# Batch norm and ReLU on one core: 32 KB runs on one queue in place of 4 KB rows on two

## Chip, core and metric

The kernel runs on one core of a Trainium2 chip. The metric is the device time of one execution in microseconds (us). Shown are the median of 13 runs and, for the views of the profile, one profiled execution.

## The reference

The input x has 32 images of 128 channels of 32 x 32 floats: 16.78 MB in, as much out. Each channel has four parameters.

```python
normalized = (x - running_mean[None, :, None, None]) / np.sqrt(running_var[None, :, None, None] + eps)
scaled = normalized * gamma[None, :, None, None] + beta[None, :, None, None]
return np.maximum(scaled, 0).astype(np.float32)
```

With scale = gamma / sqrt(var + eps) and bias = beta - mean x scale, each value becomes relu(scale x value + bias), with one scale and one bias per channel.

## The kernel before

The channel is the partition: 128 channels, 128 partitions. Two images make a tile `t` of 128 x 2 x 1024 floats (1 MB), so there are 16 tiles, and as many buffers (`BUFS`): no buffer is used twice. In DRAM a row of 1024 floats (4 KB) is one image and channel; the 128 channels of an image are neighbours, and the next image lies 512 KB further. So for each partition a tile is two separate runs of 4 KB.

The order of the work is the order of the program on each engine, and each engine that issues DMAs has a queue of its own.

- gpsimd (POOL in the profile) issues four loads of the parameter vectors, 512 bytes each, into the single row `prow` (L63 to L66).
- sync (SP) issues the load of tile 0 in two halves, and, in the main loop, those of the tiles 2, 4, 6 and 8 to 15. scalar (ACT) issues tiles 1, 3, 5 and 7 first of all, tile 1 in two halves. All of them go through `emit_input` (L53, the DMA at L58).
- TensorE turns each parameter row into a column of 128 partitions with a matmul against a single 1.0 (L79); ScalarE takes the square root (L89), and VectorE makes `scale_t` and `bias_t`, 128 x 1 each (L97 to L103).
- ScalarE then does one activation per tile of 128 x 2048 (L138) and issues that tile's store itself (L145). Tile 0 is cut finer: its first image in pieces of 256 and 768 columns, its second image whole, each with its own store (`relu_store`, L109 and L118).

A scale or bias operand of an activation is one column of 128 values, one per partition, and holds for the whole row of that instruction.

Of the kernel before, what the change touches and what calls it, by code (L numbers as in the profile page):

```python
# [1 line left out]

# [4 lines left out]


@with_exitstack
def kernel(  # L10
    ctx: ExitStack,
    tc: tile.TileContext,
    x: bass.AP,
    gamma: bass.AP,
    beta: bass.AP,
    running_mean: bass.AP,
    running_var: bass.AP,
    eps: bass.AP,
    out: bass.AP,
):  # L20
    nc = tc.nc

    B, C, H, W = x.shape
    HW = H * W
    assert C == nc.NUM_PARTITIONS, f"expected {nc.NUM_PARTITIONS} channels, got {C}"

    x3 = x.rearrange("b c h w -> b c (h w)")
    out3 = out.rearrange("b c h w -> b c (h w)")

    f32 = mybir.dt.float32  # L30

    NBMAX = 2
    n_tiles = B // NBMAX
    sizes = [NBMAX] * n_tiles
    scalar_tiles = (1, 3, 5, 7)
    splits = {0: 2, 1: 2}
    BUFS = 16
    SEPARATE_PSUM = True
    FIRST_PIECES = (256, HW - 256)

    params = ctx.enter_context(tc.tile_pool(name="params", bufs=1))
    eps_t = params.tile([C, 1], f32)
    nc.vector.memset(eps_t, float(eps))  # L43
    prow = params.tile([1, 4 * C], f32)
    one_t = params.tile([1, 1], f32)
    nc.vector.memset(one_t, 1.0)  # L46

    data = ctx.enter_context(tc.tile_pool(name="data", bufs=BUFS))
    tiles = {}
    for i in (0,) + scalar_tiles:  # L50
        tiles[i] = data.tile([C, NBMAX, HW], f32, name="t")

    def emit_input(i, t, engine):  # L53
        nsp = splits.get(i, 1)
        step = NBMAX // nsp
        b0 = i * NBMAX
        for j in range(nsp):
            engine.dma_start(  # L58
                out=t[:, j * step : (j + 1) * step],
                in_=x3[b0 + j * step : b0 + (j + 1) * step].transpose([1, 0, 2]),  # L60
            )

    nc.gpsimd.dma_start(out=prow[0:1, 3 * C : 4 * C], in_=running_var[None, :])  # L63
    nc.gpsimd.dma_start(out=prow[0:1, 0 * C : 1 * C], in_=gamma[None, :])  # L64
    nc.gpsimd.dma_start(out=prow[0:1, 2 * C : 3 * C], in_=running_mean[None, :])  # L65
    nc.gpsimd.dma_start(out=prow[0:1, 1 * C : 2 * C], in_=beta[None, :])  # L66

    emit_input(0, tiles[0], nc.sync)
    for i in scalar_tiles:
        emit_input(i, tiles[i], nc.scalar)  # L70

    pp = ctx.enter_context(tc.tile_pool(name="pp", bufs=1, space=bass.MemoryType.PSUM))
    if SEPARATE_PSUM:
        pcols = [pp.tile([C, 1], f32, name=f"p{k}") for k in range(4)]
    else:
        pc = pp.tile([C, 4], f32)
        pcols = [pc[:, k : k + 1] for k in range(4)]
    for k in (3, 0, 2, 1):
        nc.tensor.matmul(  # L79
            pcols[k],  # L80
            prow[0:1, k * C : (k + 1) * C],
            one_t[0:1, 0:1],
            start=True,
            stop=True,
        )
    g_col, b_col, mu_col, var_col = pcols

    std_t = params.tile([C, 1], f32)
    nc.scalar.activation(  # L89
        out=std_t,  # L90
        in_=var_col,
        func=mybir.ActivationFunctionType.Sqrt,
        bias=eps_t[:, 0:1],
        scale=1.0,
    )
    rstd_t = params.tile([C, 1], f32)
    nc.vector.reciprocal(out=rstd_t, in_=std_t)  # L97
    scale_t = params.tile([C, 1], f32)
    nc.vector.tensor_mul(out=scale_t, in0=g_col, in1=rstd_t)  # L99
    ms_t = params.tile([C, 1], f32)  # L100
    nc.vector.tensor_mul(out=ms_t, in0=mu_col, in1=scale_t)  # L101
    bias_t = params.tile([C, 1], f32)
    nc.vector.tensor_sub(out=bias_t, in0=b_col, in1=ms_t)  # L103

    out_ring = {}
    n_out = [0]

    def relu_store(t, b, img, c0, c1):
        nc.scalar.activation(  # L109
            out=t[:, img : img + 1, c0:c1],  # L110
            in_=t[:, img : img + 1, c0:c1],
            func=mybir.ActivationFunctionType.Relu,
            bias=bias_t[:, 0:1],
            scale=scale_t[:, 0:1],
        )
        eng = out_ring.get(n_out[0], nc.scalar)
        n_out[0] += 1
        eng.dma_start(  # L118
            out=out3[b : b + 1, :, c0:c1].transpose([1, 0, 2]),
            in_=t[:, img : img + 1, c0:c1],  # L120
        )

    for i, nb in enumerate(sizes):
        b0 = i * NBMAX
        if i in tiles:
            t = tiles.pop(i)
        else:
            t = data.tile([C, NBMAX, HW], f32, name="t")
            emit_input(i, t, nc.sync)
        if i == 0:  # L130
            c0 = 0
            for w in FIRST_PIECES:
                relu_store(t, b0, 0, c0, c0 + w)
                c0 += w
            for img in range(1, nb):
                relu_store(t, b0 + img, img, 0, HW)
        else:
            nc.scalar.activation(  # L138
                out=t[:, :nb],
                in_=t[:, :nb],  # L140
                func=mybir.ActivationFunctionType.Relu,
                bias=bias_t[:, 0:1],
                scale=scale_t[:, 0:1],
            )
            nc.scalar.dma_start(out=out3[b0 : b0 + nb].transpose([1, 0, 2]), in_=t[:, :nb])  # L145


# [1 line left out]
_INS = ['x', 'gamma', 'beta', 'running_mean', 'running_var', 'eps']  # L149
_OUTS = [((32, 128, 32, 32), 'float32')]  # L150
#: Inputs that are plain numbers.
_NUMBERS = {'eps': 1e-05}


# [26 lines left out]
```

## Time and profile before

| | us |
|---|---|
| median of 13 runs (lowest, highest) | 86.53 (86.44, 86.95) |
| the profiled execution, its whole time | 86.53 |
| its span, first to last event of the core | 84.7 |
| ScalarE, 15 activations of 128 x 2048, mean of one | 2.084 |
| loads issued by SP and by ACT | 13 and 5 |
| stores issued by ACT | 18 |

How to read the page: busy times of the engines are shares of the span; two lines then cut the span into 40 slices of 2.1 us, with the busy share of the 16 DMA engines in tenths and the GB/s that they moved. The windows view gives the same for any stretch of the span. Queue q1 is SP's, q10 ACT's, q0 gpsimd's. A packet is one piece of a transfer as one DMA engine handles it. "us to landing" is the time from the issue of a DMA to its completion. A share above 1 of the DMA engines' time means that records of neighbouring packets overlap.

### The profile page before, as it was taken

Reading aid. Unit: us, or ns where it says so; the run is one execution under the profiler, and the core shown is the slowest. Engines: PE = TensorE matmul, PEld = TensorE weight load, DVE = VectorE, ACT = ScalarE, POOL = GpSimd, SP = SyncE. Lnnn points to the kernel's source line nnn. Section 1 sums busy time; section 2 is a strip of 40 time slices with the busy share of each in tenths; the row PEclk is TensorE's granted clock in tenths of the full one; section 3 lists DMA queues with packets and bytes.
Section 4 is the critical chain, followed back from the end, with each engine's and each line's share of the span. In section 5 each row is a group of like instructions: output and inputs, shape, how many; then the busy total and the mean of one; then the engine's idle time right before and its main releaser. Section 6 shows DMA issues by size and latency. Waiting matters only on the chain.

```text
span 84.7 us, 153 instructions
## 1 busy us (share of the span) xinstructions
PE 2.3 (3%) x8; PEld 2.0 (2%) x8; DVE 0.7 (1%) x6; ACT 34.8 (41%) x20; POOL 2.3 (3%) x8
## 2 busy tenths in 40 slices
PE   0006400000000000000000000000000000000000
PEld 0005300000000000000000000000000000000000
DVE  0001100000000000000000000000000000000000
ACT  0411479007920890000049597793978910000000
POOL 5500000000000000000000000000000000000000
DMA  1999999999999999999999999999999999999991
GB/s 23 363 408 366 420 416 420 412 414 410 402 369 420 418 421 422 421 421 420 421 423 418 423 421 420 423 420 420 423 418 425 418 420 421 421 421 418 423 423 56
DMA packets 9025, 33.57 MB, mean 396 GB/s; under 512 B 704, under 2 KB 832, under 8 KB 9024
## 3 DMA queue, kind: packets, MB, share of 16 engines
q10 hardware_dynamic: 5616, 20.97, 60.8%
q1 hardware_dynamic: 3280, 12.58, 37.0%
q0 software_dynamic: 128, 0.00, 0.1%
q14 instruction: 1, 0.01, 0.0%
HBM read 16.78 MB, written 16.78 MB: 396 GB/s over the span
## 4 chain that ended last, share of the span: by engine, by line
DMA 65%; ACT 7%; ACTq 4%; issue 3%
DMA t<-in_x_dram 65%; ACT t L138 7%; ACTq L58 2%; ACTq L145 2%
## 5 line engine op out<-in xcount | busy, mean ns | idle before, releaser
L138 ACT ACTIVATE t<-t,bias_t,scale_t 128x2048 f32<-128x2048 f32 x15 | 30.6, 2084 | 24.6 <-DMA t<-in_x_dram 22.3
L109 ACT ACTIVATE t<-t,bias_t,scale_t 128x256 f32<-128x256 f32 (+2 forms) x3 | 2.8, 950 | 2.6 <-DVE bias_t L103 2.2
L89 ACT ACT_TABLE_LOAD x1 | 1.3, 1283 | 3.3 <-issue 3.3
L79 PE MATMUL p<-one_t,prow 1*128 1x1 f32 x8 | 2.3, 354 | 7.2 <-DMA prow<-in_running_var_dram 6.6
L79 PEld LDWEIGHTS p<-one_t,prow 1*128 1x128 f32 x8 | 2.0, 306 | 7.4 <-issue 6.6
L89 ACT ACTIVATE std_t<-p,eps_t 128x1 f32<-128x1 f32 x1 | 0.3, 263 | 2.6 <-PE p L79 2.6
L63 POOL DMA_DIRECT2D prow<-in_running_var_dram x1 | 0.6, 617 | 0.8 <-POOLq L162 0.8
L66 POOL DMA_DIRECT2D prow<-in_beta_dram x1 | 0.5, 487 | 0.0
L64 POOL DMA_DIRECT2D prow<-in_gamma_dram x1 | 0.5, 484 | 0.0
L65 POOL DMA_DIRECT2D prow<-in_running_mean_dram x1 | 0.5, 484 | 0.0
L97 DVE RECIPROCAL rstd_t<-std_t 128x1 f32<-128x1 f32 x1 | 0.2, 164 | 6.6 <-ACT std_t L89 6.6
L99 DVE TENSOR_TENSOR scale_t<-p,rstd_t 128x1 f32<-128x1 f32 x1 | 0.2, 157 | 0.6 <-PE p L79 0.6
L101 DVE TENSOR_TENSOR ms_t<-p,scale_t 128x1 f32<-128x1 f32 x1 | 0.2, 157 | 0.4 <-PE p L79 0.4
L103 DVE TENSOR_TENSOR bias_t<-p,ms_t 128x1 f32<-128x1 f32 x1 | 0.2, 157 | 0.4 <-PE p L79 0.4
L162 POOL MEMSET const-float32-0.0<- 128x1 f32 x1 | 0.1, 98 | 0.2 <-issue 0.2
L162 POOL MEMSET const-bfloat16-1.0<- 128x1 bf16 x1 | 0.1, 102 | 0.0
L162 POOL MEMSET const-float32-1.0<- 128x1 f32 x1 | 0.1, 98 | 0.0
L162 POOL MEMSET const-uint8-127<- 128x1 uint8 x1 | 0.1, 98 | 0.0
L43 DVE MEMSET eps_t<- 128x1 f32 x1 | 0.1, 59 | 0.8 <-PEq L162 0.8
L46 DVE MEMSET one_t<- 1x1 f32 x1 | 0.1, 59 | 0.0
## 6 DMA issues: line engine op xcount, KB each, us to landing
out_dram<-t ACTq DMA_DIRECT2D x15, 1024.0 KB, 15.2
t<-in_x_dram SPq DMA_DIRECT2D x11, 1024.0 KB, 17.9
t<-in_x_dram ACTq DMA_DIRECT2D x3, 1024.0 KB, 16.6
t<-in_x_dram ACTq DMA_DIRECT2D x2, 512.0 KB, 6.1
t<-in_x_dram SPq DMA_DIRECT2D x2, 512.0 KB, 5.7
out_dram<-t ACTq DMA_DIRECT2D x1, 512.0 KB, 10.7
out_dram<-t ACTq DMA_DIRECT2D x1, 384.0 KB, 16.3
out_dram<-t ACTq DMA_DIRECT2D x1, 128.0 KB, 15.3
```

What stands on the lines that cost most here:

```text
L58: engine.dma_start(out=t[:, j * step : (j + 1) * step], in_=x3[b0 + j * step : b0 + (j + 1) * step].transpose([1, 0, 2]),)
L63: nc.gpsimd.dma_start(out=prow[0:1, 3 * C : 4 * C], in_=running_var[None, :])
L64: nc.gpsimd.dma_start(out=prow[0:1, 0 * C : 1 * C], in_=gamma[None, :])
L65: nc.gpsimd.dma_start(out=prow[0:1, 2 * C : 3 * C], in_=running_mean[None, :])
L66: nc.gpsimd.dma_start(out=prow[0:1, 1 * C : 2 * C], in_=beta[None, :])
L79: nc.tensor.matmul(pcols[k], prow[0:1, k * C : (k + 1) * C], one_t[0:1, 0:1], start=True, stop=True,)
L89: nc.scalar.activation(out=std_t, in_=var_col, func=mybir.ActivationFunctionType.Sqrt, bias=eps_t[:, 0:1], scale=1.0,)
L97: nc.vector.reciprocal(out=rstd_t, in_=std_t)
L109: nc.scalar.activation(out=t[:, img : img + 1, c0:c1], in_=t[:, img : img + 1, c0:c1], func=mybir.ActivationFunctionType.Relu, bias=bias_t ...
L138: nc.scalar.activation(out=t[:, :nb], in_=t[:, :nb], func=mybir.ActivationFunctionType.Relu, bias=bias_t[:, 0:1], scale=scale_t[:, 0:1],)
L145: nc.scalar.dma_start(out=out3[b0 : b0 + nb].transpose([1, 0, 2]), in_=t[:, :nb])
L162: nc = _bacc.Bacc("TRN2", target_bir_lowering=False, num_devices=1)
```

## The change

x is now seen as 4096 rows of 1024 floats, (image, channel) in one index. Sixteen neighbouring rows go to one partition, so that 2048 rows fill the 128 partitions and two such blocks (t = 0, 1) hold all of x. Each block is loaded in two pieces of eight rows per partition: 32 KB of consecutive DRAM, 4 MB over all partitions. All four loads are issued by sync at the start, each into a tile of its own; neighbouring partitions lie 64 KB apart in DRAM.

Row j of partition p has the channel (16 p + j) mod 128, so 16 rows of a partition need 16 scales and biases, and the pattern repeats after 8 partitions. The four parameter vectors are loaded by gpsimd as 8 x 16 tables into `raw`. A matrix `rep` (8 x 128, 1.0 where the partition number modulo 8 equals the row, else 0) is made by gpsimd with a memset and a select, and one matmul spreads the tables over 128 partitions (`cols`, 128 x 64). Square root, reciprocal, two products and a difference then make `scale_t` and `bias_t` of 128 x 16.

ScalarE does one activation for each row j of a tile, 128 x 1024, with column j of the tables: 32 in all. When the eight rows of a tile are done, sync stores the tile in one DMA of 4 MB.

```diff
+J = 16
+PIECES = ((0, 8), (8, 16))
...
+    xr = x.rearrange("b c h w -> (b c) (h w)").rearrange("(t p j) w -> t p j w", p=P, j=J)
+    outr = out.rearrange("b c h w -> (b c) (h w)").rearrange("(t p j) w -> t p j w", p=P, j=J)
...
+    for t in range(T):
+        for a, b in PIECES:
+            xt = data.tile([P, b - a, HW], F32, name=f"x{t}_{a}")
+            nc.sync.dma_start(out=xt, in_=xr[t, :, a:b, :])
+            tiles.append((t, a, b, xt))
...
+    raw = params.tile([Q, 4, J], F32, name="raw")
+    for k, src in enumerate((running_var, gamma, running_mean, beta)):
+        nc.gpsimd.dma_start(out=raw[:, k, :], in_=src.rearrange("(q j) -> q j", j=J))
...
+    nc.gpsimd.memset(rep, 1.0)
+    nc.gpsimd.affine_select(
+        out=rep,
+        in_=rep,
+        compare_op=mybir.AluOpType.is_equal,
+        fill=0.0,
+        base=0,
+        pattern=[[0, P // Q], [-1, Q]],
+        channel_multiplier=1,
+    )
+    cols = psum.tile([P, 4, J], F32, name="cols")
+    nc.tensor.matmul(
+        cols.rearrange("p k j -> p (k j)"),
+        rep.rearrange("q r s -> q (r s)"),
+        raw.rearrange("q k j -> q (k j)"),
+        start=True,
+        stop=True,
+    )
+    std_t = params.tile([P, J], F32, name="std_t")
+    nc.scalar.activation(out=std_t, in_=cols[:, 0, :], func=ACTF.Sqrt, bias=eps_t[:, 0:1], scale=1.0)
...
-    nc.gpsimd.dma_start(out=prow[0:1, 3 * C : 4 * C], in_=running_var[None, :])
-    nc.gpsimd.dma_start(out=prow[0:1, 0 * C : 1 * C], in_=gamma[None, :])
-    nc.gpsimd.dma_start(out=prow[0:1, 2 * C : 3 * C], in_=running_mean[None, :])
-    nc.gpsimd.dma_start(out=prow[0:1, 1 * C : 2 * C], in_=beta[None, :])
-
-    emit_input(0, tiles[0], nc.sync)
-    for i in scalar_tiles:
-        emit_input(i, tiles[i], nc.scalar)
...
-            nc.scalar.dma_start(out=out3[b0 : b0 + nb].transpose([1, 0, 2]), in_=t[:, :nb])
+    for t, a, b, xt in tiles:
+        for j in range(a, b):
+            nc.scalar.activation(
+                out=xt[:, j - a, :],
+                in_=xt[:, j - a, :],
+                func=ACTF.Relu,
+                bias=bias_t[:, j : j + 1],
+                scale=scale_t[:, j : j + 1],
+            )
+        nc.sync.dma_start(out=outr[t, :, a:b, :], in_=xt)
```

More of the change, by code (lines that the diff above doesn't have):

```diff
@@ L6 @@
 from concourse._compat import with_exitstack
+F32 = mybir.dt.float32
+ACTF = mybir.ActivationFunctionType
+J = 16
+PIECES = ((0, 8), (8, 16))
 @with_exitstack
@@ L24 @@
     HW = H * W
[L25 to L39, printed above, removed]
-    params = ctx.enter_context(tc.tile_pool(name="params", bufs=1))
@@ L42 @@
-    eps_t = params.tile([C, 1], f32)
-    nc.vector.memset(eps_t, float(eps))
[L44 to L60, printed above, removed]
-            )
@@ L63 @@
-    nc.gpsimd.dma_start(out=prow[0:1, 3 * C : 4 * C], in_=running_var[None, :])
-    nc.gpsimd.dma_start(out=prow[0:1, 0 * C : 1 * C], in_=gamma[None, :])
-    nc.gpsimd.dma_start(out=prow[0:1, 2 * C : 3 * C], in_=running_mean[None, :])
-    nc.gpsimd.dma_start(out=prow[0:1, 1 * C : 2 * C], in_=beta[None, :])
-    emit_input(0, tiles[0], nc.sync)
-    for i in scalar_tiles:
-        emit_input(i, tiles[i], nc.scalar)
-    pp = ctx.enter_context(tc.tile_pool(name="pp", bufs=1, space=bass.MemoryType.PSUM))
@@ L73 @@
[L73 to L145, printed above, removed]
+    P = nc.NUM_PARTITIONS
@@ new lines @@
+    assert C % J == 0 and P % (C // J) == 0 and (B * C) % (P * J) == 0
+    Q = C // J
+    T = B * C // (P * J)
+    xr = x.rearrange("b c h w -> (b c) (h w)").rearrange("(t p j) w -> t p j w", p=P, j=J)
+    outr = out.rearrange("b c h w -> (b c) (h w)").rearrange("(t p j) w -> t p j w", p=P, j=J)
+    data = ctx.enter_context(tc.tile_pool(name="data", bufs=1))
+    params = ctx.enter_context(tc.tile_pool(name="params", bufs=1))
+    psum = ctx.enter_context(tc.tile_pool(name="psum", bufs=1, space=bass.MemoryType.PSUM))
@@ new lines @@
+    tiles = []
+    for t in range(T):
[6 more added lines that the diff above has]
+        nc.gpsimd.dma_start(out=raw[:, k, :], in_=src.rearrange("(q j) -> q j", j=J))
+    eps_t = params.tile([P, 1], F32, name="eps_t")
@@ new lines @@
+    nc.vector.memset(eps_t, float(eps))
+    rep = params.tile([Q, P // Q, Q], F32, name="rep")
+    nc.gpsimd.memset(rep, 1.0)
[16 more added lines that the diff above has]
+    )
@@ new lines @@
+    std_t = params.tile([P, J], F32, name="std_t")
+    nc.scalar.activation(out=std_t, in_=cols[:, 0, :], func=ACTF.Sqrt, bias=eps_t[:, 0:1], scale=1.0)
+    rstd_t = params.tile([P, J], F32, name="rstd_t")
+    nc.vector.reciprocal(out=rstd_t, in_=std_t)
+    scale_t = params.tile([P, J], F32, name="scale_t")
+    nc.vector.tensor_mul(out=scale_t, in0=cols[:, 1, :], in1=rstd_t)
+    ms_t = params.tile([P, J], F32, name="ms_t")
+    nc.vector.tensor_mul(out=ms_t, in0=cols[:, 2, :], in1=scale_t)
@@ L149 @@
+    bias_t = params.tile([P, J], F32, name="bias_t")
+    nc.vector.tensor_sub(out=bias_t, in0=cols[:, 3, :], in1=ms_t)
+    for t, a, b, xt in tiles:
[6 more added lines that the diff above has]
+                scale=scale_t[:, j : j + 1],
+            )
+        nc.sync.dma_start(out=outr[t, :, a:b, :], in_=xt)
 _INS = ['x', 'gamma', 'beta', 'running_mean', 'running_var', 'eps']
```

## The prediction

> **What bounds the kernel now.** First the page: busy time by engine, the 40 slices, the queues, the chain.
>
> ```profile
> span 84.7 us, 153 instructions
> ...
> PE 2.3 (3%) x8; PEld 2.0 (2%) x8; DVE 0.7 (1%) x6; ACT 34.8 (41%) x20; POOL 2.3 (3%) x8
> ...
> DMA  1999999999999999999999999999999999999991
> GB/s 23 363 408 366 420 416 420 412 414 410 402 369 420 418 421 422 421 421 420 421 423 418 423 421 420 423 420 420 423 418 425 418 420 421 421 421 418 423 423 56
> DMA packets 9025, 33.57 MB, mean 396 GB/s; under 512 B 704, under 2 KB 832, under 8 KB 9024
> ...
> q10 hardware_dynamic: 5616, 20.97, 60.8%
> q1 hardware_dynamic: 3280, 12.58, 37.0%
> ...
> DMA t<-in_x_dram 65%; ACT t L138 7%; ACTq L58 2%; ACTq L145 2%
> ```
>
> No compute engine is busy for half the span, and the DMA row is 9 in every slice but the first and last. The chain names loads (65%). All but one of the 9,025 packets are under 8 KB: with 4 KB of contiguous DRAM per image and channel, a packet of x is 4 KB. So the bound is how fast 16 DMA engines pass 33.57 MB in 4 KB packets. The windows view says when they reach what (last two columns: DMA share, GB/s).
>
> ```profile
> 1.70:3.00 1.30, 0.00 (x0) 0.00 (x0) 0.00 (x0) 0.00 (x0) 1.30 (x4) 1.00 0.86 262
> 3.00:10.00 7.00, 2.30 (x8) 1.99 (x8) 0.64 (x4) 1.86 (x3) 0.29 (x1) 1.00 1.02 393
> 10.00:23.00 13.00, 0.00 (x0) 0.00 (x0) 0.00 (x0) 7.77 (x6) 0.00 (x0) 1.00 1.02 413
> 23.00:25.00 2.00, 0.00 (x0) 0.00 (x0) 0.00 (x0) 0.74 (x1) 0.00 (x0) 1.00 1.04 364
> 25.00:27.00 2.00, 0.00 (x0) 0.00 (x0) 0.00 (x0) 0.00 (x0) 0.00 (x0) 1.00 1.03 415
> 27.00:80.00 53.00, 0.00 (x0) 0.00 (x0) 0.00 (x0) 24.46 (x12) 0.00 (x0) 1.00 1.03 421
> 70.00:80.00 10.00, 0.00 (x0) 0.00 (x0) 0.00 (x0) 0.00 (x0) 0.00 (x0) 1.00 1.02 421
> 80.00:83.20 3.20, 0.00 (x0) 0.00 (x0) 0.00 (x0) 0.00 (x0) 0.00 (x0) 1.00 0.93 383
> 83.20:84.70 1.50, 0.00 (x0) 0.00 (x0) 0.00 (x0) 0.00 (x0) 0.00 (x0) 1.00 0.00 0
> ```
>
> These rows make an account of the span. From 1.70 to 3.00 the transfers move 262 x 1.30 = 341 KB, 0.81 us at 421 GB/s, so the flow begins, in effect, at 3.00 - 0.81 = **2.19 us**. All bytes at 421 take 33.57 MB / 421 = **79.74 us**. From 3 to 10 us, 393 for 421 loses 7 x 28/421 = **0.47 us**; from 10 to 27 us the three rows lose 0.25 + 0.27 + 0.03 = **0.55 us**. The last 3.20 us move 1,226 KB, worth 2.91 us, so the flow ends at 82.91, and **1.79 us** follow with the last receipts and the end of the program. Sum 84.74, against a span of 84.7. The profiled execution took 86.53 us, so 1.83 us lie around its span; it equals the median of the 13 runs.
>
> **The change, part by part.** *The bytes* stay: 16.78 MB in, 16.78 MB out. What changes is how they are cut. Eight neighbouring rows of 4 KB are one DRAM run of 32 KB, so 8,320 data packets (4,096 rows in, 4,096 out, and 128 rows stored in two pieces) become 1,024 if a run is one packet. Before shows no packet of that size, so I bound the fixed cost of a packet from the smaller ones it does show: the first image is stored as 256 and 768 columns, 128 packets of 1 KB and 128 of 3 KB.
>
> ```profile
> 10.31 1.28 ACTq L118 DMA_DIRECT2D out_dram<-t  x2
> ...
> out_dram<-t ACTq DMA_DIRECT2D x1, 384.0 KB, 16.3
> out_dram<-t ACTq DMA_DIRECT2D x1, 128.0 KB, 15.3
> ```
>
> Issued from 10.31 us on, they land 15.3 and 16.3 us later, near 25.6 and 27.5 us: the two windows 23-25 and 25-27. At 421 GB/s a 4 KB packet takes 16 x 4,096 / 421 = 155.7 ns of an engine. In 25-27 the 16 engines have 32 us and move 830 KB; less 393 KB in 3 KB packets that is 107 packets of 4 KB, 16.6 us, so a 3 KB packet takes 15.4 us / 128 = 120 ns. The line through 3 KB and 4 KB leaves **14 ns** fixed in each packet. The same sum for 23-25 gives 73 ns for 1 KB and 45 ns fixed, which would put the data part at 37 GB/s per engine, far off anything the slices show. So the ends are 0 (421 GB/s stays) and 14 ns (a 32 KB packet of 1,147 ns, 64 per engine, 73.4 us); an effect below zero is a rival below. I take **5 ns**, nearer to zero: the row of 421 is 53 us long, that of 415 only 2 us with loads alternating between the stores. Then a 32 KB packet takes 8 x 150.7 + 5 = 1,211 ns, and 64 of them **77.5 us** (433 GB/s): 2.2 us less than 79.74.
>
> The Trainium skill, "DMA: Bandwidth & Descriptors", section "Why small descriptors are slow (HBM only)", says that a packet carries some 3 cycles of overhead beside one cycle per 32 bytes; by that the step is (1,024 + 3) / (8 x 131) and the data time an estimated 78.1 us. The trace's 5 ns is a little more.
>
> *One queue in place of two.* The four loads stand first in SP's ring and the stores behind. I cost this at nothing: the last 10 us of before hold stores only, all on ACT's queue, at the same 421 as the mixed stretch. The ring must not run dry, though. Loads land in turn; the flow starts at 2.19, loses 0.47 early and takes 77.5 / 8 = 9.7 us per 4 MB, so at 12.4, 22.0, 31.7 and 41.4 us; the four stores' turns are at 41.4, 51.1, 60.8 and 70.5.
>
> ```profile
> L109 ACT ACTIVATE t<-t,bias_t,scale_t 128x1024 f32<-128x1024 f32 x1 | 1.2, 1239 | 0.4 <-ACT t L109 0.4
> ...
> L58 SPq DMA_DIRECT2D t<-in_x_dram x13: 367/372/625, 0.7 to 38.0; - x13
> ...
> SPq L58 <- DMA t<-in_x_dram: 28.2, 5, 9.9
> ```
>
> *ScalarE* now does 32 activations of 128x1024, since scale and bias change with the row: 8 x 1.239 = 9.9 us per tile, 39.6 in all against 34.8 before. With the parameters there in time, tiles are ready at 22.3, 32.2, 42.1 and 52.0 us, some 18 us ahead of each turn, and the transfer flow hides them. If that cover is gone, the last tile's 9.9 us is what is late.
>
> *SP's issues.* Eight at 0.37 to 0.63 us each. A store waits on SP for its eight activations; behind it on SP there are only later stores, because all loads went ahead. Before, SP waited 28.2 us for landings ahead of new loads. Should the same hold up the fourth load until the first has landed (12.4), loads two and three still cover 19 us. The first load again has 128 runs and starts at 0.7 us, so I keep 2.19. ACT issues no DMA any more; that was beside the flow.
>
> *The parameters.* POOL issues its four loads, then a memset and a select for the 8x128 matrix of ones and zeros; one matmul, one square root and four short vector operations follow.
>
> ```profile
> prow<-in_running_var_dram POOLq DMA_DIRECT2D x1, 0.5 KB, 5.3
> ...
> prow<-in_beta_dram POOLq DMA_DIRECT2D x1, 0.5 KB, 6.0
> ...
> 2.80 0.49 POOL L66 DMA_DIRECT2D prow<-in_beta_dram  x1
> ...
> 9.49 0.16 DVE L103 TENSOR_TENSOR bias_t<-p,ms_t 128x1 f32<-128x1 f32 x1 [0.44 <-PE p L79]
> ```
>
> Before, the last vector lands at 2.80 + 6.0 = 8.8 us and the bias is done at 9.65. Now these crumbs share the engines with packets of 1.21 us. If nothing scales with the packet they land at 8.8, if everything does at 2.80 + 8 x 6.0 = 50.8. I take an estimate in between, nearer to the first: four vectors, each a data packet and a completion, each behind one 32 KB packet, add 8 x 1.21 = 9.7 us: 18.5, and with 2 us for the chain (it was 0.85) the bias at **20.5 us**. With 1.4 us for a store's issue and first bytes, the last store comes late once the bias is later than 70.5 - 39.6 - 1.4 = **29.5 us**, the first from 41.4 - 9.9 - 1.4 = 30.1. The margin is 9 us, and the estimate costs nothing.
>
> *The losses.* The small store pieces go, and with them the mixed stretch: I drop the 0.55 us and keep the 0.47. At the end each engine finishes on a packet of 1.21 us rather than 0.16; I add **0.3 us** for engines that finish apart.
>
> **The sum:** 2.19 + 77.5 + 0.47 + 0.3 + 1.79 + 1.83 = 84.1; with part of the early loss going along with the 4 KB packets, **84.0 us**, 2.9% faster.
>
> **The rivals.** *A, the forecast*: fixed cost per packet spread over 32 KB. For it: the pieces of 3 KB ran at 415 and those of 1 KB at 364. Its own range is 82.4 to 85.2; the far end of 14 ns would give 80.0, to which I give 0.02.
>
> *B, the runs don't become cheaper packets* (cut into small ones by the hardware, or 421 is the limit of the path): 2.19 + 79.74 + 0.47 + 0.3 + 1.79 + 1.83 = **86.3**, or 85.5 with both small losses gone. For it: loads, stores and mixtures all stop at 421, as a common limit would.
>
> *C, slower: the parameter vectors starve behind 32 KB packets.* Place: the wait for the vectors ahead of the matmul. It decides from a bias later than 29.5 us; each us beyond costs one, the gain of 2.5 us is gone at 32, and landing wholly in proportion (50.8, bias at 52.8) makes the last store start at 93.8, so 93.8 + 9.7 + 0.3 + 1.79 + 1.83 = **107 us**. For it: each crumb needed 5.3 us even behind small packets. Against it: some of that 5.3 us is descriptor making and latency, which don't grow.
>
> The Trainium skill, same page, section "Queues, rings and completion order", has each engine go round the queues a whole packet at a time, which is the mechanism of C; no row here shows it with long packets.
>
> *D, slower: the DRAM pattern.* Neighbouring partitions now read 64 KB apart instead of 4 KB, all engines at offsets that are equal powers of two, and could meet in the memory. If the rate were that of the poorest long stretch in the trace, 393 GB/s, the data would take 85.4 us: 2.19 + 85.4 + 0.3 + 1.79 + 1.83 = **91.5**. It decides from a data time of 79.9 us, 420 GB/s. Against it: loads and stores of before, also 4 KB apart in powers of two, run at 421 without a dip.
>
> The Trainium skill's same page, section "Latency and other measured facts", reports a loss for large power-of-two row pitches, 207 instead of 214 GB/s at 512 KB and worse beyond; at that 3% the forecast would come to an estimated 86.6. It gives nothing for 64 KB.
>
> **How the numbers follow.** A 0.64, beyond its fast end 0.02, B 0.18, C 0.07, D 0.09. The range from 82.4 to 86.4 holds A, nearly all of B and little of D: 0.8. Faster by more than 0.2% (about what a measurement of this kernel can tell from no change; below 86.36): A, its end, most of B, a little of D, 0.79. Within: 0.07. Slower: C and most of D, 0.14.
>
> **What would show it.** Right: about 1,024 data packets and slices of 430 or more from 10 us to the end, without a dip at 41 us where loads turn to stores; 32 activations done near 60 us; bias before 29 us. B: slices at 421, or 8,000 packets. C: a hole in the DMA row near 42 us and ScalarE waiting for the bias. D: loads or stores under 415 with the share still at 1. If the ring were not served in order, stores would land among the loads; that alone changes no time. The forecast fails most easily on the 5 ns, for which no long packet of before stands.

## The result and the profile after

The changed kernel takes 84.65 us (median of 11 runs, 84.50 to 84.86), the one before 86.54 us: the ratio on record is 0.9774, with a 95% interval from 0.9758 to 0.9789 (the plain quotient of these two medians is 0.978). The forecast was 84.0 us. The profiled execution took 84.77 us.

The page of the changed kernel: busy times, slices, packets, queues and the chain.

```profile
span 83.1 us, 117 instructions
...
PE 0.7 (1%) x2; PEld 0.5 (1%) x2; DVE 0.8 (1%) x5; ACT 38.0 (46%) x34; POOL 3.0 (4%) x10
...
DMA  7788996998999699889969999997999899799980
GB/s 205 300 379 379 505 490 268 505 505 363 395 505 489 300 473 505 379 379 505 252 268 489 473 394 394 505 442 331 489 473 410 379 505 442 331 489 489 394 379 0
DMA packets 1280, 33.56 MB, mean 404 GB/s; under 512 B 256, under 2 KB 256, under 8 KB 256
...
q1 hardware_dynamic: 1152, 33.55, 95.8%
...
DMA x<-in_x_dram 50%; ACT x L92 10%; SPq L50 1%; ACTq L130 1%
```

Of 1,280 packets 256 are small (parameters and completions), so 1,024 carry x: one packet per run of 32 KB. The ragged GB/s row is no ragged flow: the 16 engines start their packets close together (within 0.4 us before the turn to stores, 0.7 us after it), a round of packets is 16 x 32 KB = 524 KB, and a slice holds between one and two rounds (505 GB/s x 2.08 us is two of them). Longer windows average most of this out. Three of them, around the place where loads turn to stores; the last column is GB/s:

```profile
20.00:38.00 18.00, 0.00 (x0) 0.00 (x0) 0.00 (x0) 18.00 (x17) 0.00 (x0) 1.00 1.01 437
38.00:43.00 5.00, 0.00 (x0) 0.00 (x0) 0.00 (x0) 5.00 (x5) 0.00 (x0) 1.00 0.96 308
43.00:76.00 33.00, 0.00 (x0) 0.00 (x0) 0.00 (x0) 9.56 (x9) 0.00 (x0) 1.00 1.00 430
```

The rows of 437 and 430 are one and the same flow: 18 us hold 14.8 rounds and the window counts 15. By the packets' own 1,213 ns it is 432 GB/s for loads and stores alike, instead of 421, as the forecast said. But between 38 and 43 us it falls to 308, which the forecast had excluded. The timeline shows that no store was late:

```profile
0.82 1.88 SPq L50 DMA_DIRECT2D x<-in_x_dram  x4
...
3.00 0.52 POOL L57 DMA_DIRECT2D raw<-in_beta_dram  x1
...
15.94 0.17 DVE L88 TENSOR_TENSOR bias_t<-cols,ms_t 128x16 f32<-128x16 f32 x1
16.15 36.48 ACT L92 ACTIVATE x<-x,bias_t,scale_t 128x1024 f32<-128x1024 f32 x32 [1.03 <-DVE bias_t L88]
25.33 27.65 SPq L99 DMA_DIRECT2D out_dram<-x  x4
```

All loads are issued by 2.70 us, the bias is done at 16.1 us, the 32 activations end at 52.6 us, and the first store is issued at 25.33 us, some 16 us before its turn.

The trace also holds each packet with its start and duration. Of the 1,024, 960 take exactly 1,213 ns. Two groups take longer: the first 16, one per engine (0.60 us per engine), and the last 32 of the 512 load packets, so the **last two load packets** of each engine ahead of its first store packet (1.25 us per engine). (A record names no engine; that the packets are shared evenly is taken from their order.) This gives the account of the span: first packet at 1.82, plus 0.60, plus 64 x 1.213 = 77.6, plus 1.25, makes 81.3 us for an average engine (the last packets end at 81.4 on average); the slowest ends at 81.8, and 1.3 us follow to the end of the span.

### The profile page after: what moved, and what is told of

The parts are those of the page before. It is cut to its first block, busy times and chain, and to the rows that moved or that the text cites. A ratio compares the mean times of both kernels' runs of the same rounds, so it can differ in the third digit from the quotient of the medians.

```text
span 83.1 us, 117 instructions
## 1 busy us (share of the span) xinstructions
PE 0.7 (1%) x2; PEld 0.5 (1%) x2; DVE 0.8 (1%) x5; ACT 38.0 (46%) x34; POOL 3.0 (4%) x10
## 2 busy tenths in 40 slices
DMA packets 1280, 33.56 MB, mean 404 GB/s; under 512 B 256, under 2 KB 256, under 8 KB 256
## 4 chain that ended last, share of the span: by engine, by line
DMA 50%; ACT 10%; SPq 1%; ACTq 1%; issue 0%
DMA x<-in_x_dram 50%; ACT x L92 10%; SPq L50 1%; ACTq L130 1%
## 5 line engine op out<-in xcount | busy, mean ns | idle before, releaser
L92 ACT ACTIVATE x<-x,bias_t,scale_t 128x1024 f32<-128x1024 f32 x32 | 36.4, 1226 | 1.1 <-DVE bias_t L88 1.0
L72 PE MATMUL cols<-raw,rep 8*128 8x64 f32 x2 | 0.7, 428 | 14.2 <-DMA raw<-in_beta_dram 14.2
L57 POOL DMA_DIRECT2D raw<-in_running_var_dram x1 | 0.7, 675 | 0.8 <-POOLq L116 0.8
L72 PEld LDWEIGHTS cols<-raw,rep 8*128 8x128 f32 x2 | 0.5, 306 | 14.1 <-issue 14.1
L57 POOL DMA_DIRECT2D raw<-in_beta_dram x1 | 0.5, 521 | 0.0
L57 POOL DMA_DIRECT2D raw<-in_gamma_dram x1 | 0.5, 518 | 0.0
L57 POOL DMA_DIRECT2D raw<-in_running_mean_dram x1 | 0.5, 518 | 0.0
```

The source lines that it names most:

```text
L57: nc.gpsimd.dma_start(out=raw[:, k, :], in_=src.rearrange("(q j) -> q j", j=J))
L72: nc.tensor.matmul(cols.rearrange("p k j -> p (k j)"), rep.rearrange("q r s -> q (r s)"), raw.rearrange("q k j -> q (k j)"), start=True, s ...
L92: nc.scalar.activation(out=xt[:, j - a, :], in_=xt[:, j - a, :], func=ACTF.Relu, bias=bias_t[:, j : j + 1], scale=scale_t[:, j : j + 1],)
```

## The experiments

Three questions: does the gain come from the length of the packets or from the order and the single queue; what is the loss at the first store; and how near is the parameter load to hurting. Each run is compared with the kernel before on the same chip.

### Length of the packet against order and queue

**Packets of 4 KB (e1) and 8 KB (e2).** A gap of 64 bytes after every row, or every two rows, of the tile in the core's memory splits each DMA; the DRAM addresses, the order and the queue stay. The edit of e1 is shown for the loads; the activations and stores index the tile in the same way, and e2 has `G = 2`.

```diff
+G = 1
...
-            xt = data.tile([P, b - a, HW], F32, name=f"x{t}_{a}")
-            nc.sync.dma_start(out=xt, in_=xr[t, :, a:b, :])
+            xt = data.tile([P, (b - a) // G, G * HW + 16], F32, name=f"x{t}_{a}")
+            nc.sync.dma_start(out=xt[:, :, : G * HW], in_=xr[t, :, a:b, :].rearrange("p (g r) w -> p g (r w)", r=G))
...
```

> Only the length of a packet is undone: the tiles are padded by 64 bytes after every row of 4 KB, so that each DMA falls into 4 KB pieces; queue, order, DRAM addresses, size of the DMAs, tables and activations stay those of the changed kernel. Theory P (a fixed cost in every packet, 1213 ns for 32 KB against 8 x 155.7): data time 512 x 155.7 ns = 79.7 us instead of 64 x 1.213 = 77.6, so 84.65 + 2.1 = 86.8 us, ratio to before about 1.003. Rival Q (the gain comes from one queue, from loads ahead of stores or from larger DMAs): stays at 84.65, ratio 0.978. On the parameters: if they wait for whole packets of the load queue, they land 6 to 7 us after their issue again instead of 11.0.

> The same with padding after every two rows: packets of 8 KB. Theory P, with 4.7 ns fixed and 151.0 ns per 4 KB: a packet of 306.7 ns, 256 per engine, 78.5 us, so 84.65 + 0.9 = 85.5 us, ratio 0.989. Rival Q: 84.65, ratio 0.978.

**Runs of 16 KB (e8) and 64 KB (e10).** Here the pieces themselves change, and with them the size of a DMA (2 MB and 8 MB).

```diff
-PIECES = ((0, 8), (8, 16))
+PIECES = ((0, 4), (4, 8), (8, 12), (12, 16))
```

```diff
-PIECES = ((0, 8), (8, 16))
+PIECES = ((0, 16),)
```

> The changed kernel with four pieces of four rows per block instead of two of eight: runs of 16 KB, eight loads and eight stores of 2 MB. Fixed cost per packet (4.7 ns and 151.0 ns per 4 KB): 128 packets of 608.7 ns, 77.9 us, 0.3 more than with 32 KB. If the loss at the first store follows the packet (1.25 us at 32 KB, 0.36 at 8 KB by the runs so far), it falls to some 0.65: 84.65 + 0.3 - 0.6 = 84.35 us. If it doesn't depend on the packet: 84.95 us. The parameters should land some 8 us after their issue, between the 7.0 of 8 KB packets and the 11.0 of 32 KB.

> One piece of 16 rows per block: runs of 64 KB, two loads and two stores of 8 MB. If a run is one packet: 32 packets of 2417 ns, 77.3 us of data time, 0.3 less than with 32 KB. If the loss at the turn goes with the length of the load packets, it grows from 1.25 us to about 2: 84.65 - 0.3 + 0.8 = 85.2 us; if not, 84.35 us. The parameters wait for packets twice as long: each later vector some 4.8 us behind the one before, the last one near 20 us instead of 14, the bias near 22 us; the first store's turn is near 41 us and its 16 activations take 18 us, so it is just in time.

Measured: e1 85.96 us, ratio 0.9923 (0.9901 to 0.9945); e2 84.93 us, 0.9803 (0.9766 to 0.9840); e8 84.70 us, 0.9776 (0.9748 to 0.9805); e10 86.02 us, 0.9946 (0.9932 to 0.9960). The packets' own records, in an extract that adds up their durations beyond the commonest one and divides by the 16 engines:

```
run     data packets      commonest   extra at the start   extra at the first store
e1      8,192 of  4 KB      159 ns        0.64 us               0.0 us
e2      4,096 of  8 KB      309 ns        0.49 us               0.36 us
e8      2,048 of 16 KB      611 ns        0.58 us               0.82 us
after   1,024 of 32 KB    1,213 ns        0.60 us               1.25 us
e10       512 of 64 KB    2,418 ns        0.63 us               (no flow to turn)
```

The column of durations is a straight line: (2,418 - 1,213) / 8 = 150.6 ns for 4 KB and 8 ns fixed in each record. Records of neighbours overlap a little: at 421 GB/s packets of 4 KB follow each other every 155.7 ns, so about 5 ns of the fixed part is paid. The starts of the packets in the steady stretch of the stores say the same: 155.4, 306, 608 and 1,210 ns from one to the next at 4, 8, 16 and 32 KB leave 4.7 ns fixed. From 4 KB to 32 KB that is 79.7 - 77.6 = 2.1 us of data time. But e1 is only 1.3 us slower than the change. The change pays 1.25 us at its turn from loads to stores, where e1 pays nothing; e1 in return has longer records while it loads, 0.42 us per engine in all between 10 and 44 us. The sum is 2.1 - 1.25 + 0.42 = 1.27 us. The same three windows of e1, e2 and e8, in that order:

```profile
20.00:38.00 18.00, 0.00 (x0) 0.00 (x0) 0.00 (x0) 16.20 (x15) 0.00 (x0) 1.00 1.02 416
38.00:43.00 5.00, 0.00 (x0) 0.00 (x0) 0.00 (x0) 4.82 (x5) 0.00 (x0) 1.00 1.02 415
43.00:76.00 33.00, 0.00 (x0) 0.00 (x0) 0.00 (x0) 9.16 (x8) 0.00 (x0) 1.00 1.02 422
```

```profile
20.00:38.00 18.00, 0.00 (x0) 0.00 (x0) 0.00 (x0) 16.63 (x16) 0.00 (x0) 1.00 1.01 426
38.00:43.00 5.00, 0.00 (x0) 0.00 (x0) 0.00 (x0) 4.11 (x4) 0.00 (x0) 1.00 1.01 393
43.00:76.00 33.00, 0.00 (x0) 0.00 (x0) 0.00 (x0) 9.16 (x8) 0.00 (x0) 1.00 1.01 428
```

```profile
20.00:38.00 18.00, 0.00 (x0) 0.00 (x0) 0.00 (x0) 18.00 (x17) 0.00 (x0) 1.00 1.00 429
38.00:43.00 5.00, 0.00 (x0) 0.00 (x0) 0.00 (x0) 5.00 (x6) 0.00 (x0) 1.00 1.02 364
43.00:76.00 33.00, 0.00 (x0) 0.00 (x0) 0.00 (x0) 5.72 (x6) 0.00 (x0) 1.00 1.01 431
```

Read down the middle rows: 415, 393, 364, and 308 for the change. What longer packets win in the steady flow they partly give back at the turn. From 16 to 32 KB the two cancel: e8 has 0.4 us more of data time and 0.4 us less at the turn, and its time is the change's. So both theories held a part: packet length is worth 1.3 us net, and the rest of the gain, 0.67 us, is there in e1 with packets of 4 KB. It comes with the new order, the single queue and the larger DMAs together, which were not separated, and no row says where in the span it lies.

**The kernel before without its small store pieces (e11).** This tests the rows from which the forecast had drawn its fixed cost.

```diff
-    FIRST_PIECES = (256, HW - 256)
+    FIRST_PIECES = (HW,)
```

> The kernel before, with the first image stored whole: no packets of 1 KB and 3 KB any more. My sum booked 0.27 + 0.03 us of its loss in the windows from 23 to 27 us, where these packets run: 86.53 - 0.3 = 86.2 us, ratio 0.9965. If that dip belongs to the first stores of the execution and not to their small packets, 86.5 us, ratio 1.000.

Measured 86.83 us, ratio 1.0033 (1.0015 to 1.0052): slightly slower, not faster. Windows of e11:

```profile
18.00:22.00 4.00, 0.00 (x0) 0.00 (x0) 0.00 (x0) 0.00 (x0) 0.00 (x0) 1.00 1.01 402
22.00:24.00 2.00, 0.00 (x0) 0.00 (x0) 0.00 (x0) 0.00 (x0) 0.00 (x0) 1.00 0.99 342
24.00:27.00 3.00, 0.00 (x0) 0.00 (x0) 0.00 (x0) 1.73 (x1) 0.00 (x0) 1.00 1.03 425
```

No packet of x is below 4 KB here, and the dip is still there, 342 GB/s. It stands where the first stores begin (the first store packet starts at 23.5 us), and small packets aren't needed for it. In the packets' records it is 0.32 us per engine between 22 and 24 us, so the order and queues of before lose time at this place with packets of 4 KB too, where e1 loses none.

### The loss at the first store

**More turns (e3).** The fourth load is issued behind the first store.

```diff
-            nc.sync.dma_start(out=xt, in_=xr[t, :, a:b, :])
+            if (t, a) != (1, 8):
+                nc.sync.dma_start(out=xt, in_=xr[t, :, a:b, :])
...
         nc.sync.dma_start(out=outr[t, :, a:b, :], in_=xt)
+        if (t, a) == (0, 0):
+            nc.sync.dma_start(out=tiles[3][3], in_=xr[1, :, 8:16, :])
```

> One queue as in the changed kernel, but the fourth load is issued behind the first store, so the ring turns three times between loads and stores instead of once (load, load, load, store, load, store, store, store). ScalarE is ready ahead of each store's turn by the durations measured. Theory T (each turn in a ring costs some 1.2 us of every engine): 2 more turns, 84.65 + 2.4 = 87.0 us. Rival N (the dip near 40 us is no property of the turn, but a single event or a matter of how packets are recorded): 84.65 us.

Measured 84.89 us, 0.9792 (0.9758 to 0.9827). In the packets' records the first change from loads to stores costs 1.16 us per engine, the second 0.19, the change back nothing. Theory T, a price for every turn, falls.

**Two rings (e4).** The stores go to the scalar queue, so that loads and stores stand in two rings (a ring is the list of a queue's waiting transfers).

```diff
-        nc.sync.dma_start(out=outr[t, :, a:b, :], in_=xt)
+        nc.scalar.dma_start(out=outr[t, :, a:b, :], in_=xt)
```

> The stores of the changed kernel are issued on the scalar queue instead of the sync queue; loads and stores of 32 KB packets then alternate from about 26 us on, and no ring turns. Theory T, if the turn costs only within a ring: 84.65 - 1.2 = 83.4 us. If it costs whenever an engine goes from a load packet to a store packet, dozens of turns: over 100 us. Rival N: 84.65 us.

Measured 84.30 us (84.19 to 84.37, 4 runs), 0.9725 (0.9690 to 0.9759): the fastest of all, each of its runs below each run of the change, though those were timed at another time and the two intervals overlap by a hair. The loss is not gone: 1.01 us per engine, again on the two load packets ahead of the first store packet of each engine, although the store stands in another ring. After it, 32 KB load and store packets alternate at 1,213 ns without loss. So the loss belongs to neither ring nor to alternation.

**An early small store (e5).** Row 0 of the first tile goes out by itself on the scalar queue.

```diff
+            if (t, j) == (0, 0):
+                nc.scalar.dma_start(out=outr[0, :, 0:1, :], in_=xt[:, 0:1, :])
-        nc.sync.dma_start(out=outr[t, :, a:b, :], in_=xt)
+        lo = 1 if (t, a) == (0, 0) else 0
+        nc.sync.dma_start(out=outr[t, :, a + lo : b, :], in_=xt[:, lo:, :])
```

> Row 0 of the first tile is stored by itself on the scalar queue as soon as it is done (about 18 us, 4 KB packets, 512 KB in all); the other seven rows of the tile follow on the sync queue as before. The runs so far put the loss of some 1.2 us once per execution, on the last two load packets ahead of the first store packet, and a second turn of the ring cost only 0.2 us. Theory W (the first store of an execution costs it, whatever its size and place): the loss is taken early by a small store and may shrink, and the dip near 40 us is gone: 83.5 to 84.65 us, the last two 32 KB load packets ahead of 41 us at 1.21 us each. Theory L (an engine looks two packets ahead, and the loss is about the length of the long packets at the change from loads to stores): the dip near 40 us stays, 84.65 us.

**A first store of short packets (e7).**

```diff
-        nc.sync.dma_start(out=outr[t, :, a:b, :], in_=xt)
+        step = 1 if (t, a) == (0, 0) else 8
+        for r in range(0, 8, step):
+            nc.sync.dma_start(out=outr[t, :, a + r : a + r + step, :], in_=xt[:, r : r + step, :])
```

> The mirror of it: the loads keep 32 KB packets, the first store is issued as eight DMAs of one row per partition, 4 KB packets (again 0.26 us). Theory L, store packets set the loss: 84.65 + 0.26 - 1.1 = 83.8 us; load packets set it: 84.9 us. Theory W: 84.9 us.

**A last load of short packets: 4 KB (e6), and with `step = 2` 8 KB (e12).**

```diff
-            nc.sync.dma_start(out=xt, in_=xr[t, :, a:b, :])
+            step = 1 if (t, a) == (1, 8) else 8
+            for r in range(0, 8, step):
+                nc.sync.dma_start(out=xt[:, r : r + step, :], in_=xr[t, :, a + r : a + r + step, :])
```

> The fourth load is issued as eight DMAs of one row per partition, packets of 4 KB; the first store still has 32 KB packets. Cutting 4 MB into 4 KB packets costs 64 x 155.7 - 8 x 1213 = 0.26 us. Theory L in the form that the load packets at the change set the loss: 84.65 + 0.26 - 1.1 = 83.8 us. In the form that the store packets set it: 84.65 + 0.26 = 84.9 us. Theory W: 84.9 us.

> The fourth load in four DMAs of two rows, packets of 8 KB; the other loads and all stores keep 32 KB. In the run with the fourth load in 4 KB packets the loss at the turn fell from 1.25 to 0.3 us of each engine, but the short packets took some 0.8 us more than long ones. Packets of 8 KB cost 32 x 309 - 8 x 1213 = 0.2 us. If the loss goes with the length of the packets that the engine has been loading for the last 10 us: 0.36 at the turn, 84.65 + 0.2 - 0.9 = 83.95 us, which would beat the 84.3 of the two rings. If what counts is something else of the first store: 84.85 us.

**Only the last row in short packets (e9).**

```diff
-            nc.sync.dma_start(out=xt, in_=xr[t, :, a:b, :])
+            for lo, hi in ((a, 15), (15, 16)) if (t, a) == (1, 8) else ((a, b),):
+                nc.sync.dma_start(out=xt[:, lo - a : hi - a, :], in_=xr[t, :, lo:hi, :])
```

> Of the fourth load only the last row of each partition is split off as a DMA of its own: seven rows in packets of 28 KB, then eight packets of 4 KB per engine ahead of the first store. It costs some 0.1 us of data time. Theory L with a look-ahead counted in packets (two packets ahead of the first store): the loss at the turn falls from 1.25 us per engine to about the 0.3 of the run with the whole load in 4 KB packets, 84.65 + 0.1 - 0.95 = 83.8 us. Look-ahead counted in bytes (some 32 to 64 KB): half of the loss stays, 84.2 us. Theory W (first store, whatever stands before it): 84.75 us.

The five together, with the extra from the packets' records as above:

```
run     edit                                  time      ratio (95%)                extra at the turn
after                                         84.65     0.9774 (0.9758 to 0.9789)    1.25 us
e5      row 0 stored early, 4 KB packets      84.87     0.9800 (0.9769 to 0.9831)    1.02 us
e7      first store in 4 KB packets           85.01     0.9817 (0.9788 to 0.9845)    1.07 us
e6      last load (10 us) in 4 KB packets     84.70     0.9787 (0.9757 to 0.9817)    0.29 us
e12     last load in 8 KB packets             84.86     0.9794 (0.9771 to 0.9817)    0.79 us
e9      last row (1.2 us) in 4 KB packets     85.36     0.9870 (0.9854 to 0.9886)    1.33 us
```

Theory W, that a first store of any kind pays, falls with e5: its small store was issued at 17.5 us, and the big turn still costs 1.02 us; the 4 KB store packets themselves ran between the loads from 21.0 to 30.7 us, with 0.05 us of extra on the loads. That the store packets set the loss falls with e7. The loads do bear on it, since ten microseconds of 4 KB packets bring it down to 0.29. But the length of the very last ones doesn't: in e9 eight packets of 4 KB per engine stand ahead of the store, and they take nearly the whole loss themselves (1.19 of the 1.33 us). And with 8 KB packets in the last load alone (e12) 0.79 us are left, more than the 0.36 of an execution with 8 KB throughout. None of the five is faster than the change: in e6 the gain at the turn is used up by the short packets (64 x 159 - 8 x 1,213 ns = 0.47 us more, and another 0.36 us of long ones between 32 and 38 us). **What the engine does in that time stays open**; shown is only its place, its size, that it is paid in full only once (the second turn of e3 costs 0.19 us), and that it goes with the length of the packets loaded before it. e6 and e12, with ten microseconds of short packets, stay above e1 and e2, so more than the last ten seem to count. Length isn't all of it, as e11 shows.

### How near the parameters are

Landing times of the four vectors, from the pages of the change and of e1, in us after their issue (last column):

```profile
raw<-in_running_var_dram POOLq DMA_DIRECT2D x1, 0.5 KB, 6.6
raw<-in_gamma_dram POOLq DMA_DIRECT2D x1, 0.5 KB, 8.4
raw<-in_running_mean_dram POOLq DMA_DIRECT2D x1, 0.5 KB, 10.3
raw<-in_beta_dram POOLq DMA_DIRECT2D x1, 0.5 KB, 11.0
```

```profile
raw<-in_running_var_dram POOLq DMA_DIRECT2D x1, 0.5 KB, 5.2
...
raw<-in_beta_dram POOLq DMA_DIRECT2D x1, 0.5 KB, 4.9
```

Only the packets beside them differ. With the issues at 1.32, 1.99, 2.50 and 3.00 us, the change's vectors land at 7.9, 10.4, 12.8 and 14.0 us; the first three are 2.4 us apart, two packets of 1.21. The records show the turns themselves: the small packets of gpsimd's queue run in seven rounds, at 6.0, 7.2, 8.5, 9.7, 10.9, 12.1 and 13.3 us, with one 32 KB packet of each engine between two rounds. With 64 KB (e10) the DMA issues, the timeline and a window, in this order, show what rival C describes:

```profile
raw<-in_beta_dram POOLq DMA_DIRECT2D x1, 0.5 KB, 19.9
```

```profile
24.80 0.17 DVE L88 TENSOR_TENSOR bias_t<-cols,ms_t 128x16 f32<-128x16 f32 x1
25.01 36.30 ACT L92 ACTIVATE x<-x,bias_t,scale_t 128x1024 f32<-128x1024 f32 x32 [1.02 <-DVE bias_t L88]
43.24 18.44 SPq L99 DMA_DIRECT2D out_dram<-x  x2
```

```profile
41.20:43.20 2.00, 0.00 (x0) 0.00 (x0) 0.00 (x0) 2.00 (x3) 0.00 (x0) 1.00 0.00 0
```

The last vector lands at 3.00 + 19.9 = 22.9 us, the bias is done at 25.0, and the 16 activations of the first tile end at 43.2 us, when the loads have been through for over 1.6 us. Two microseconds show 0 GB/s; by the packets' records the hole is 2.5 us, and it is why e10 loses to the change although its data time is 0.3 us shorter. I had expected it to be just in time.

## Why the prediction was right, and by how much it was off

- **The forecast's mechanism** was right, and its main term nearly exact: 64 packets of 1,211 ns forecast, 1,213 measured. Rival B, 421 GB/s as a limit of the path, falls: the flow runs at 432. By the Trainium skill, "DMA: Bandwidth & Descriptors", section "Why small descriptors are slow (HBM only)", the data time was an estimated 78.1 us; the measured 77.6 is nearer to the forecast's 77.5.
- **The evidence for that term was weak.** I drew the far end of 14 ns, and the support for a fixed cost, from the windows of 25-27 and 23-25 us of before, taking the dip for that of small packets. e11 has the dip without them. The packets' records of before had the answer all along: 46, 121 and 159 ns at 1, 3 and 4 KB, which is 37.6 ns per KB and 8 ns fixed, the straight line of the experiments. The 120 ns that I worked out for 3 KB was right; the 73 ns for 1 KB was not, because packets of 4 KB beside them were longer by 0.25 us per engine. The 5 ns was thus a choice near zero and no reading, though the prediction once calls it the trace's, and that it was met so closely is in part luck. e1, e2, e8 and e10 are the measurement that it needed.
- **One queue, loads ahead of stores, "at nothing":** this step failed. Steady rates of loads, of stores and of mixtures were all in the trace, and I took from them that the change between them is free. It costs 1.25 us per engine with packets of 32 KB. This is the term that was missing. It is more than the whole difference between a span of 82.2 and one of 83.1 us, because other terms were booked too high.
- **The dropped 0.55 us** was a real loss, but not that of the small pieces: the records of before are longer by 0.49 us per engine between 10 and 27 us, 0.31 of it between 21 and 25 around the first stores, and e11 has 0.55 without the pieces. The change has none of it before its turn, and there its own, larger loss. e1, 0.67 us faster than before, still has 0.42 while it loads, so its gain is for the most part something else.
- **The other terms.** Start and early loss: 2.19 + 0.47 = 2.66 us forecast, 1.82 + 0.60 = 2.42 measured. Engines that finish apart and the end of the span: 0.3 + 1.79 = 2.09 forecast, 0.5 + 1.3 = 1.8 measured. These 0.5 us too many hide part of the missing 1.25, so that the total came within 0.65 us is in part luck too.
- **ScalarE and the parameters** were hidden as forecast, with more to spare: the bias at 16.1 us where I had 20.5. I had booked eight whole packets behind one another for the four vectors; the steps of 2.4 us fit two packets per vector, but the waits overlapped in part, in seven rounds. The tiles that I had ready from 22.3 us on left out that bias of 20.5, by which the first is ready at 30.4; the first store was issued at 25.3. The Trainium skill's rule in "DMA: Bandwidth & Descriptors", section "Queues, rings and completion order", that an engine takes its queues in turn, a whole packet at a time, agrees with the rounds 1.21 us apart, with one run of 32 KB as the packet.
- **Rival C** did not decide here, but it is real: at 64 KB it does, from a bias of 25 us, with 16 rather than 8 activations ahead of the first store.
- **Rival D**, the DRAM pattern: falls. Loads and stores run at 432 GB/s with partitions 64 KB apart. The Trainium skill's loss at large power-of-two pitches ("DMA: Bandwidth & Descriptors", section "Latency and other measured facts") does not show at this one.

## What to carry to other kernels

Where a kernel is bound by DMA, longer contiguous runs save a fixed cost per packet, here some 5 ns, 2.6% of the data time from 4 KB to 32 KB, and most of it is had by 16 KB; beyond that, everything that is paid by the packet, a turn from loads to stores or a small transfer that waits for its slot, eats the rest. Steady rates from a profile don't price the moment between two steady states: look for a row that contains the change itself, or keep a term for it. And a dip that stands beside a suspect is no evidence until the suspect has been taken away alone, or until the records of the single packets have been read.

## What the hardware showed that was not expected

- **The loss at the first store**, above: in full once per execution, on the last load packets of each engine (two of 32 KB, three of 16 KB), 0 to 1.25 us per engine as the packets of the changed kernel go from 4 to 32 KB, in one ring or in two.
- **A store can hold its engine's issue for microseconds.** The rows of the stores' issue in e1 (4 KB packets) and in the change, duration min/median/max in ns:

```profile
L100 SPq DMA_DIRECT2D out_dram<-x x4: 6847/7078/7295, 22.7 to 52.9; - x4
```

```profile
L99 SPq DMA_DIRECT2D out_dram<-x x4: 332/338/344, 25.3 to 52.6; - x4
```

A DMA of 4 MB takes 7 us to issue as 1,024 pieces of 4 KB, and 0.34 us as 128 pieces of 32 KB. It is not the pieces alone: the first two loads of e1, on an empty queue, were issued in 0.43 and 0.57 us, and the third and fourth, behind them, took 8.3 and 9.8 us. Here SP had nothing else to do.
